# Reading the moving columns of matmuls in reverse order, with the weight tiles' places spread over 32 relations

## The chip, the cores and the metric

The kernel runs on one core of one Trainium2 chip. The metric is the device time of one execution in microseconds, as the median of several runs.

## What is computed

One decoder layer over 272 tokens (16 meta tokens and 256 of the sequence), 2048 channels wide. The part that the change touches is the feed-forward block at the end, which takes about two thirds of the time:

```python
def conv_gated_ffn(h, w_up, conv_w, conv_b, w_down):
    T = h.shape[1]
    z = h @ w_up
    zp = jnp.pad(z, ((0, 0), (CONV_WIDTH - 1, 0), (0, 0)))
    z = sum(zp[:, j:j + T] * conv_w[j] for j in range(CONV_WIDTH)) + conv_b
    a, g = jnp.split(z, 2, axis=-1)
    return (jax.nn.gelu(a) * g) @ w_down
```

`w_up` is 2048 x 11264 and `w_down` 5632 x 2048. Ahead of it stand the projections, a sparse attention, a pooling branch and an output projection, and layer norms (in `reference`: `h = layer_norm(ALPHA * h + f, ...)`).

## The kernel before

All large products run on TensorE in float32r. Each float32 operand is split into an upper part and a lower part, and a product is the sum of three matmuls: upper with upper, and each lower with the other's upper. So a block of weights of 128 x 128 costs three matmuls, and each of them loads its stationary block anew.

**Weights.** All weight tiles of 128 x 2048 come in one stream (`stream`), in the order in which they are used, each by one DMA of 1 MB into a `wraw` buffer (three of them). ScalarE writes the upper parts into a `whl` buffer (L181) and VectorE the lower parts (L182); there are three `whl` buffers of 4288 float32 places per partition. The tiles are fetched two ahead of use. Where the two parts lie in the `whl` buffer is set by a pair of places per tile (`Split`), and these set the relation of the addresses of the stationary blocks to those of the columns that stream past them. `turned` says whether the second matmul of a block takes the lower weights or the lower activations.

**Lead.** A tile that has a `lead` is stored in two pieces, the first 512 columns (four blocks) at other places than the rest, and is split by two instructions on each engine, one of 512 columns and one of 1536. A tile without one is split by two instructions of 1024 columns. Before the change every up tile has the lead `LEAD_H = (12, False)`: its first four blocks begin at place 12 in the order not turned, and its other twelve lie, counted modulo 256 bytes, 48 bytes ahead of that (place 0), in turned order.

**Up tiles.** One up tile is 128 output channels: 16 blocks, 48 matmuls, in `product` (L288 for the first of each three, L292 for the other two). The weights are stationary; the 258 columns of the normalised activations (`hp`, upper and lower parts in fixed buffers) are moving, and the result is 128 x 258 in a PSUM bank. There are 88 up tiles. The first eight work on activations before their norm (`fold`, 260 columns); the other 80 on `hp`, which makes 3840 matmuls.

**Down tiles.** In `seven` (L890 to L892) the gated activations are stationary and 512 columns of the `whl` tile are moving. Seven products of sums of blocks take the place of eight. Tiles of kind A have four products of three matmuls, tiles of kind B three; `j` counts the pairs of channel tiles that are summed in PSUM. Up and down tiles alternate from about 420 to 960 us of the span, in the order of `ffn_plan`. The scheduler of the language fixes the order of instructions on each engine when the kernel is built.

Of the kernel before, what the change touches and what calls it, by code (L numbers as in the profile page):

```python
# [23 lines left out]
NQ = T - Q0  # L24
KT = D // P
# [11 lines left out]
FOLDED = 4  # L37
# [63 lines left out]
LEAD_X, LEAD_H = (24, False), (12, False)  # L101


def lead(b):

    return LEAD_H


GATED, RIGHT, FOLD = 0, 32, 32
# [20 lines left out]
K_UP = (1, 3, 5, 7, 8, 10, 12, 15, 0, 2, 4, 6, 9, 11, 13, 14)  # L130
# [3 lines left out]
def tile_layer(ctx, tc, xt, w_first, w_proj, w_uk, w_uv, w_pool, w_o, w_up, w_down, cols, rows, rel_bias, onehot, out):  # L134
    nc = tc.nc
# [10 lines left out]
    def small():  # L146
        return pa.tile([P, 512], F32, tag="at", name="at")
# [3 lines left out]
    ps = small()  # L151
# [4 lines left out]
    stream = [w_proj[j] for j in range(8)] + [w_uk, w_uv] + [w_proj[j] for j in range(8, 24)]  # L156
    stream += [w_o[j] for j in range(KT)]
    plan = ffn_plan()
    kinds, leads, downs_at = {}, {**{i: LEAD_X for i in range(10, 18)}, **{26 + m: LEAD_H for m in (0, 1, 5)}}, {}
    for item in plan:  # L160
        if item[0] == "up":
            leads[len(stream)] = lead(2 * item[1] + item[2])
            stream.append(w_up[item[2] * FT + item[1]])
        elif item[0] == "down":
            n = PARTS[FAST]
            stream.append(w_down[sum(PARTS[:FAST]) + n // 2 + (item[2] - 1) // 2 * (n // 4) + item[3]])
        else:
            kinds[len(stream)] = item[0]
            downs_at[len(stream)] = down(item[0])
            stream.append(w_down[sum(PARTS[:item[1]]) + item[2] * (PARTS[item[1]] // 2) + item[3]])  # L170
# [3 lines left out]
    ready, raws, split, held = {}, {}, {}, []  # L174
# [103 lines left out]
        nc.scalar.activation(hi, total.to_broadcast([P, 2]), AF.Copy)  # L278
        nc.vector.tensor_tensor(lo, total.to_broadcast([P, 2]), hi.bitcast(F32), op=ALU.subtract)

    def product(ps, hl, act, lo, hi, places, ks=None, k0=0, k1=KT):

        for n in range(k0, k1):
            k = (places if ks is None else ks)[n]
            w = slice(P * places.index(k), P * places.index(k) + P)
            wh, wl = hl[:, 0, w], hl[:, 1, w]
            ah, al = act[k][:, 0, lo:hi], act[k][:, 1, lo:hi]
            nc.tensor.matmul(ps, wh, ah, start=n == 0, stop=False)  # L288
            turned = hl.early if hl.lead is not None and w.start < LEAD else hl.turned
            turn = ((wl, ah), (wh, al)) if turned else ((wh, al), (wl, ah))  # L290
            for i, (a, b) in enumerate(turn):
                nc.tensor.matmul(ps, a, b, start=False, stop=i == 1 and n == KT - 1)  # L292
# [6 lines left out]
    for k0, k1 in [(k, k + 1) for k in range(9)] + [(9, 12), (12, 15), (15, 16)]:  # L299
# [6 lines left out]
        if k0 % 6 == 0:  # L306
            hl = split_tile()
# [57 lines left out]
    ps = heads[0][0]  # L365
# [22 lines left out]
    for j in range(2):  # L388
        ps = heads[1 + j][0]
# [6 lines left out]
    ps = small()  # L396
# [482 lines left out]
    def seven(kind, part, c, j):  # L879

        hl = weights()
        n = PARTS[part] // 2
        names = (("P2", 2), ("P3", 3), ("P1", 0), ("P5", 1)) if kind == "A" else (("P7", 1), ("P6", 0), ("P4", 2))
        if j == 0:
            for name, _ in names:
                held[name] = small()
        for name, w in names:
            a, i = pairs[part][j][name]
            ps, w = held[name], slice(512 * w, 512 * w + 512)
            nc.tensor.matmul(ps, a[:, 0, i], hl[:, 0, w], start=j == 0, stop=False)  # L890
            nc.tensor.matmul(ps, a[:, 0, i], hl[:, 1, w], start=False, stop=False)  # L891
            nc.tensor.matmul(ps, a[:, 1, i], hl[:, 0, w], start=False, stop=j == n - 1)  # L892
        if j < n - 1:
            return
        c11, c12, c21, c22 = (y2[:, i, w:w + 512] for i in range(2) for w in (512 * c, 1024 + 512 * c))

        def add(to, ps):

            with tc.issue_after(split[min(state["use"] + 1, last - 1)][1]):
                nc.vector.scalar_tensor_tensor(to, to, 1.0 if part else ALPHA, ps, op0=ALU.mult, op1=ALU.add)  # L900

        if kind == "A":
            held["u"] = fp.tile([P, 512], F32, name="u", tag="u1", bufs=1, padded_shape=[P, NQ + W])
            nc.scalar.activation(held["u"], held["P1"], AF.Copy)
            held["v"] = fp.tile([P, 512], F32, name="v", tag="u2", bufs=1, padded_shape=[P, NQ + W])
            nc.scalar.activation(held["v"], held["P5"], AF.Copy)
            add(c11, held["P2"])
            add(c12, held["P3"])
            nc.gpsimd.dma_start(c11, held["u"], accum_op=ALU.add)
            nc.gpsimd.dma_start(c12, held["v"], accum_op=ALU.add)  # L910
        else:
            u, v = held["u"], held["v"]
            add(c22, v)
            nc.vector.tensor_tensor(u, u, held["P6"], op=ALU.add)  # L914
            nc.vector.tensor_tensor(v, u, held["P7"], op=ALU.add)
            add(c21, held["P4"])
            nc.gpsimd.dma_start(c12, u, accum_op=ALU.add)
            nc.gpsimd.dma_start(c21, v, accum_op=ALU.add)
            nc.gpsimd.dma_start(c22, v, accum_op=ALU.add)
# [4 lines left out]
    for item in plan:  # L924
        if item[0] in "AB":
            seven(*item)
            continue
        if item[0] == "down":
            _, part, c, g = item
            hl = weights()  # L930
            if c == 1:
                emit((last, spare)[g])
                if g == 0:
                    row_sums(last, ready[last])
            if g == 0:
                downs = [big(), big()]
            n = PARTS[part]
            for k in range(4 * g, 4 * g + 4):
                w = slice(512 * (k - 4 * g), 512 * (k - 4 * g) + 512)
                for i in range(2):  # L940
                    a, r = pairs[part][k // 2][f"a{i + 1}{k % 2 + 1}"]
                    nc.tensor.matmul(downs[i], a[:, 0, r], hl[:, 0, w], start=k == 0, stop=False)
                    nc.tensor.matmul(downs[i], a[:, 0, r], hl[:, 1, w], start=False, stop=False)
                    nc.tensor.matmul(downs[i], a[:, 1, r], hl[:, 0, w], start=False, stop=k == n - 1)
            if g == n // 4 - 1:
                for i in range(2):
                    yc = y2[:, i, 512 * c:512 * c + 512]
                    nc.vector.tensor_tensor(yc, yc, downs[i], op=ALU.add)
            continue
        _, f, half_ = item  # L950
        part = next(p for p in range(len(PARTS)) if f < sum(PARTS[:p + 1]))
        if half_ == 0:
            if f % 2 == 0:
                pair = fp.tile([P, 2, S], F32, name="za", tag="z0", bufs=3)
            both = []
        hl = weights()
        ps = big()

        b = 2 * (f - FOLDED) + half_
        upper, lower = split[state["use"] + 1]  # L960
        with tc.issue_after(lower):
            for m in turns[:(0, 5, 5, 6)[b] if 0 <= b < 4 else 0]:
                nc.vector.transpose(y[:, m, NM:], y[:, m, NM:])
                turns.remove(m)
        with tc.issue_after(upper):
            for _ in range(0 if b < 4 else 4 if b < 8 else 3):
                if moves:
                    residual(*moves.pop(0))
        if todo and f > FOLDED + half_:
            p, r = todo.pop(0)  # L970
            with behind(state["use"]):
                pairs[p].append(forms(r, len(pairs[p]), p == FAST))
        if f < FOLDED:
            k = 0
            if f + half_ == 0:
                product(ps[:, :NE], hl, folded, 0, NE, K_UP, k1=5)
                deviation()
                k = 5
            product(ps[:, :NE], hl, folded, 0, NE, K_UP, k0=k)
            with behind(state["use"]):  # L980
                while len(h_parts) < min(KT, 2 * (2 * f + half_ + 1) + 1):
                    normalise(len(h_parts))
            both.append(ps)
            if half_ == 0:
                continue
            both = [conv(i * FT + f, i, unfold(both[i]), pair[:, f % 2]) for i in range(2)]
        else:
            product(ps[:, :NQ], hl, h_parts, 0, NQ, K_UP, ks=late_last if f == FOLDED else None)
            both.append(conv(half_ * FT + f, half_, ps, pair[:, f % 2]))
            if half_ == 0:  # L990
                continue
        gate(*both)
        if part > FAST:
            a = fp.tile([P, 2, WIDE], F32R, name="gp", tag="gp", bufs=16)
            gated.append(two_parts(a[:, :, :S], both[0]))
        elif f % 2:
            todo.append((part, pair))
# [192 lines left out]
```

## Time and profile before

| | us |
|---|---|
| median of 2 runs | 1027.88 (1027.29 to 1028.48) |
| profiled execution | 1027.44 |
| its span, first to last instruction | 1025.6 |
| TensorE busy in the span | 1018.5 |
| VectorE busy | 890.5 |
| ScalarE busy | 620.1 |

The span is what the profile's rows are counted in; 1.8 us of the profiled time lie outside it. Matmuls overlap one another in the pipeline, so that the length of a single one in a row (0.28 us for 258 columns) is not what it costs. What it costs is the distance from its start to the start of the next one. In the timeline a row that ends in "x2" holds two instructions that follow one another.

### The profile page before, as it was taken

To read this page: it belongs to the slowest core of one execution; us is meant where nothing else is said; L and a number is where in the kernel's file an instruction comes from. 1 tells how busy PE (TensorE), PEld (TensorE's weight loads), DVE (VectorE), ACT (ScalarE), POOL (GpSimd) and SP (SyncE) were. 2 spreads that over 40 slices of the span, in tenths; PEclk is the share of its full clock that TensorE was granted. 3 is DMA by queue.
4 is the path that set the end of the run, shared out by engine and by line. 5 is a ranking of instruction groups with operands and counts; after the bars stand their busy time and mean duration, and the time that the engine had idled before them with its cause. 6 is when DMAs were issued, how large, how long until landed. Compare 5 with 4: busy or idle time off the path is not lost.

```text
span 1025.6 us, 19201 instructions
## 1 busy us (share of the span) xinstructions
PE 1018.5 (99%) x7644; PEld 969.4 (95%) x7644; DVE 890.5 (87%) x1401; ACT 620.1 (60%) x1000; POOL 188.4 (18%) x245
## 2 busy tenths in 40 slices
PE   9999999999999999999999999999999999999997
PEld 8999999999999999999999999999999999999986
DVE  6878668758879998999998989989899999999876
ACT  7666446645448856555666565566556656666675
POOL 1200014125430131111121111210212102120031
PEclk9999999999999999999999999999999999999998
DMA  8755643455564578979887788888888789788874
GB/s 328 257 184 206 228 154 108 138 197 168 203 205 134 189 229 249 278 283 296 281 288 259 270 275 278 277 279 298 278 272 279 292 295 289 266 290 286 290 244 138
DMA packets 59754, 250.28 MB, mean 244 GB/s; under 512 B 21734, under 2 KB 22416, under 8 KB 32656
## 3 DMA queue, kind: packets, MB, share of 16 engines
q1 hardware_dynamic: 34592, 230.42, 62.8%
q0 software_dynamic: 7888, 16.14, 8.3%
q10 hardware_dynamic: 17184, 2.49, 1.5%
q8 instruction: 60, 0.98, 0.4%
q14 instruction: 30, 0.25, 0.1%
HBM read 232.50 MB, written 2.11 MB: 229 GB/s over the span
## 4 chain that ended last, share of the span: by engine, by line
PE 71%; DVE 12%; DMA 8%; issue 4%; ACT 4%; POOL 1%; POOLq 0%; ACTq 0%; SPq 0%; DVEq 0%
PE mm L292 36%; PE mm L288 18%; DVE whl L182 6%; DMA wraw<-in_w_up 4%; DMA wraw<-in_w_down 4%; ACT whl L181 3%; PE at L891 3%; PE at L892 3%; PE at L890 3%; PE mm L363 2%; DVE y L900 1%; DVE wraw L198 1%; DVE wraw L197 1%; DVE gp L845 0%; DVE wraw L193 0%
## 5 line engine op out<-in xcount | busy, mean ns | idle before, releaser
L182 DVE TENSOR_TENSOR whl<-wraw,whl 128x1024 fp32r<-128x1024 f32 (+2 forms) x416 | 488.3, 1201 | 53.8 <-ACT whl L181 52.4
L181 ACT ACTIVATE whl<-wraw 128x1024 fp32r<-128x1024 f32 (+2 forms) x416 | 402.4, 1015 | 192.8 <-DVE wraw L198 52.1
L292 PE MATMUL mm<-hp,whl 128*128 128x258 f32 x2560 | 454.0, 280 | 0.0
L292 PEld LDWEIGHTS mm<-hp,whl 128*128 128x128 f32 x2560 | 390.9, 188 | 3.5 <-DVE whl L182 0.2
L288 PE MATMUL mm<-hp,whl 128*128 128x258 f32 x1280 | 357.6, 279 | 0.0
L288 PEld LDWEIGHTS mm<-hp,whl 128*128 128x128 f32 x1280 | 241.4, 189 | 3.1
L292 PE MATMUL mm<-xp,whl 128*128 128x256 f32 (+5 forms) x768 | 140.4, 282 | 0.0
L292 PEld LDWEIGHTS mm<-xp,whl 128*128 128x128 f32 x768 | 118.7, 189 | 0.5
L288 PE MATMUL mm<-xp,whl 128*128 128x256 f32 (+5 forms) x384 | 111.9, 292 | 0.0
L863 POOL TENSOR_TENSOR forms<-za 128x128 f32<-128x128 f32 x20 | 20.3, 1015 | 297.5 <-DVE za L839 234.5
L288 PEld LDWEIGHTS mm<-xp,whl 128*128 128x128 f32 x384 | 72.3, 188 | 1.0 <-issue 0.5
L891 PE MATMUL at<-whl,gp 128*128 128x512 f32 x180 | 70.7, 393 | 0.0
L892 PE MATMUL at<-whl,gp 128*128 128x512 f32 x180 | 70.6, 393 | 0.0
L890 PE MATMUL at<-whl,gp 128*128 128x512 f32 x180 | 68.8, 392 | 0.3 <-DVE u L914 0.3
L866 POOL TENSOR_TENSOR forms<-za 128x128 f32<-128x128 f32 x20 | 20.2, 1010 | 202.3 <-DVE za L839 190.2
L821 ACT ACTIVATE z<-mm,cv 128x256 f32<-128x256 f32 x40 | 22.3, 559 | 42.5 <-PE mm L292 42.2
L292 PE MATMUL mm<-fold,whl 128*128 128x260 f32 x256 | 45.6, 280 | 0.0
L292 PE MATMUL mm<-mixp,whl 128*128 128x258 f32 x256 | 45.5, 279 | 0.0
L292 PE MATMUL mm<-mixa,whl 128*128 128x258 f32 x256 | 45.2, 278 | 0.0
L821 ACT ACTIVATE za<-mm,cv 128x256 f32<-128x256 f32 x40 | 22.3, 558 | 35.0 <-PE mm L292 33.8
L892 PEld LDWEIGHTS at<-whl,gp 128*128 128x128 f32 x180 | 33.8, 188 | 7.4
L890 PEld LDWEIGHTS at<-whl,gp 128*128 128x128 f32 x180 | 33.5, 187 | 7.2 <-DVE u L914 1.0
(339 smaller groups left out, 1610.1 us busy)
## 6 DMA issues: line engine op xcount, KB each, us to landing
wraw<-in_w_up SPq DMA_DIRECT2D x88, 1024.0 KB, 5.2
wraw<-in_w_down SPq DMA_DIRECT2D x80, 1024.0 KB, 6.5
wraw<-in_w_proj SPq DMA_DIRECT2D x24, 1024.0 KB, 5.2
wraw<-in_w_o SPq DMA_DIRECT2D x16, 1024.0 KB, 4.9
y<-v POOLq DMA_DIRECT2D x27, 256.0 KB, 8.4
y<-u POOLq DMA_DIRECT2D x18, 256.0 KB, 5.0
wraw<-in_w_first SPq DMA_DIRECT2D x8, 304.0 KB, 5.2
x<-in_xt SPq DMA_DIRECT2D x1, 2176.0 KB, 7.8
```

Source lines behind the costliest of these rows:

```text
L181: upper = nc.scalar.activation(hl[:, 0, c], raw[:, c], AF.Copy)
L182: lower = nc.vector.tensor_tensor(hl[:, 1, c], raw[:, c], hl[:, 0, c].bitcast(F32), op=ALU.subtract)
L197: nc.vector.tensor_tensor(b12, b22, b12, op=ALU.subtract)
L288: nc.tensor.matmul(ps, wh, ah, start=n == 0, stop=False)
L292: nc.tensor.matmul(ps, a, b, start=False, stop=i == 1 and n == KT - 1)
L363: nc.tensor.matmul(ps[:m, :T], hl[:, t // 2, a0 + a:a0 + a + m], x_parts[k][:, t % 2, :], start=k == 0 and t == 0, stop=k == KT - 1 and t ...
L821: nc.scalar.activation(z, src[:, 2:NQ], AF.Identity, bias=col(C_B, j), scale=col(C_W, 3 * j + 2))
L863: nc.gpsimd.tensor_tensor(s[:, 0], a21, a22, op=ALU.add)
L866: nc.gpsimd.tensor_tensor(s[:, 3], a11, a21, op=ALU.subtract)
L890: nc.tensor.matmul(ps, a[:, 0, i], hl[:, 0, w], start=j == 0, stop=False)
L891: nc.tensor.matmul(ps, a[:, 0, i], hl[:, 1, w], start=False, stop=False)
L892: nc.tensor.matmul(ps, a[:, 1, i], hl[:, 0, w], start=False, stop=j == n - 1)
```

## The change

The change does three things, in the feed-forward block alone.

1. The 80 up tiles on `hp` read their moving columns from the last to the first, and write the columns of PSUM from the last to the first (`back=True`). The result in PSUM is the same, column by column.
2. The down tiles of odd `j` (the second and fourth pair of each four) do the same with their 512 columns: 378 matmuls.
3. Up tiles lose their lead. Tile number `b` has its upper part at place 4 x (b mod 16) and its lower part 2112 places further, in steps of 16 bytes, and 16 tiles in turned order are followed by 16 in the other. So 32 combinations come in turn; the eight tiles on `fold` get them too, and read forwards as before.

```diff
-def lead(b):
-
-    return LEAD_H
+def placed(b):
+
+    return 4 * (b % 16), 4 * (b % 16) + 2112, b // 16 % 2 == 0
...
         if item[0] == "up":
-            leads[len(stream)] = lead(2 * item[1] + item[2])
+            downs_at[len(stream)] = placed(2 * item[1] + item[2])
...
-    def product(ps, hl, act, lo, hi, places, ks=None, k0=0, k1=KT):
+    def product(ps, hl, act, lo, hi, places, ks=None, k0=0, k1=KT, back=False):
...
             ah, al = act[k][:, 0, lo:hi], act[k][:, 1, lo:hi]
+            if back:
+                ah, al = ah[:, ::-1], al[:, ::-1]
...
+        step = 1 - j % 2 * 2
         for name, w in names:
             a, i = pairs[part][j][name]
-            ps, w = held[name], slice(512 * w, 512 * w + 512)
-            nc.tensor.matmul(ps, a[:, 0, i], hl[:, 0, w], start=j == 0, stop=False)
-            nc.tensor.matmul(ps, a[:, 0, i], hl[:, 1, w], start=False, stop=False)
-            nc.tensor.matmul(ps, a[:, 1, i], hl[:, 0, w], start=False, stop=j == n - 1)
+            ps, w = held[name][:, ::step], slice(512 * w, 512 * w + 512)
+            nc.tensor.matmul(ps, a[:, 0, i], hl[:, 0, w][:, ::step], start=j == 0, stop=False)
+            nc.tensor.matmul(ps, a[:, 0, i], hl[:, 1, w][:, ::step], start=False, stop=False)
+            nc.tensor.matmul(ps, a[:, 1, i], hl[:, 0, w][:, ::step], start=False, stop=j == n - 1)
...
-            product(ps[:, :NQ], hl, h_parts, 0, NQ, K_UP, ks=late_last if f == FOLDED else None)
+            product(ps[:, NQ - 1::-1], hl, h_parts, 0, NQ, K_UP, ks=late_last if f == FOLDED else None, back=True)
```

The number of instructions stays the same on every engine, and the DMA queue's order does not change. What moves is where the split of an up tile is cut, and with it which matmul waits for the second piece. On VectorE, in the middle of the feed-forward block (near 656 us of the span), where `v<-u,at` is a sum of a down tile and `whl<-wraw,whl` the lower parts of a weight tile, the kernel before has:

```order
L915 TENSOR_TENSOR v<-u,at 128x512 [waits DMASW2_49,DMASW4_49,DMASW1_49,DVE_49]
L182 TENSOR_TENSOR whl<-wraw,whl 128x512 [waits DMAHW1_49,Activation_49]
L182 TENSOR_TENSOR whl<-wraw,whl 128x1536 [waits Activation_49]
L845 TENSOR_TENSOR gp<-za,gp 128x256 [waits Activation_49]
L845 TENSOR_TENSOR gp<-forms,gp 128x256 [waits Activation_49]
```

and the changed one, whose lines stand two or three further down:

```order
L918 TENSOR_TENSOR v<-u,at 128x512 [waits DMASW2_49,DMASW4_49,DMASW1_49,DVE_49]
L182 TENSOR_TENSOR whl<-wraw,whl 128x1024 [waits DMAHW1_49,Activation_49]
L182 TENSOR_TENSOR whl<-wraw,whl 128x1024 [waits Activation_49]
L847 TENSOR_TENSOR gp<-za,gp 128x256 [waits Activation_49]
L847 TENSOR_TENSOR gp<-forms,gp 128x256 [waits Activation_49]
```

The two pieces of the split have other sizes and stand in the same place. On TensorE, in the up tile that uses this split (the `hp` numbers are the blocks' activations), the kernel before waits for the second piece at the fifth block:

```order
L288 MATMUL mm_7917<-hp_4092,whl_7812 128x258
L292 MATMUL mm_7917<-hp_4092,whl_7812 128x258 x2
L288 MATMUL mm_7917<-hp_4098,whl_7812 128x258 [waits Activation_49]
L292 MATMUL mm_7917<-hp_4098,whl_7812 128x258 [waits DVE_49]
L292 MATMUL mm_7917<-hp_4098,whl_7812 128x258
```

and the changed one at the ninth:

```order
L290 MATMUL mm_7917<-hp_4411,whl_7812 128x258
L294 MATMUL mm_7917<-hp_4411,whl_7812 128x258 x2
L290 MATMUL mm_7917<-hp_3859,whl_7812 128x258 [waits Activation_49]
L294 MATMUL mm_7917<-hp_3859,whl_7812 128x258
L294 MATMUL mm_7917<-hp_3859,whl_7812 128x258 [waits DVE_49]
```

The wait for the second piece has moved four blocks back, and the first piece, which the tile's first matmul waits for, has grown from 512 to 1024 columns. In the changed tile the lower weights come with the third matmul of a block, which is the order that is not turned.

## Rows read from the trace of the kernel before

**Rows 1.** The page: span, busy time of the engines, TensorE's clock, up tiles' matmuls.

```profile
span 1025.6 us, 19201 instructions
PE 1018.5 (99%) x7644; PEld 969.4 (95%) x7644; DVE 890.5 (87%) x1401; ACT 620.1 (60%) x1000; POOL 188.4 (18%) x245
PEclk9999999999999999999999999999999999999998
L182 DVE TENSOR_TENSOR whl<-wraw,whl 128x1024 fp32r<-128x1024 f32 (+2 forms) x416 | 488.3, 1201 | 53.8 <-ACT whl L181 52.4
L292 PE MATMUL mm<-hp,whl 128*128 128x258 f32 x2560 | 454.0, 280 | 0.0
L288 PE MATMUL mm<-hp,whl 128*128 128x258 f32 x1280 | 357.6, 279 | 0.0
```

**Rows 2.** Stretches: length, busy us (instructions) of PE, PEld, DVE, ACT, POOL, clock, DMA.

```profile
500.00:600.00 100.00, 100.00 (x730) 94.44 (x730) 92.76 (x127) 59.45 (x83) 16.47 (x20) 1.00 0.83 276
800.00:900.00 100.00, 100.00 (x726) 94.21 (x725) 96.19 (x133) 61.06 (x88) 16.05 (x20) 1.00 0.83 284
420.00:960.00 540.00, 539.57 (x3916) 508.44 (x3916) 504.11 (x694) 325.64 (x458) 87.41 (x105) 1.00 0.85 282
```

**Rows 3.** Timeline of TensorE, one up tile: start us, length us, what.

```profile
601.07 0.28 PE L288 MATMUL mm<-hp,whl 128*128 128x258 f32 x1
...
601.42 0.28 PE L288 MATMUL mm<-hp,whl 128*128 128x258 f32 x1
...
602.50 0.28 PE L288 MATMUL mm<-hp,whl 128*128 128x258 f32 x1
...
603.57 0.28 PE L288 MATMUL mm<-hp,whl 128*128 128x258 f32 x1
...
606.34 0.28 PE L288 MATMUL mm<-hp,whl 128*128 128x258 f32 x1
...
606.69 0.39 PE L890 MATMUL at<-whl,gp 128*128 128x512 f32 x1
```

**Rows 4.** Timeline of TensorE: first matmuls of an output projection tile and its successor.

```profile
248.55 0.28 PE L288 MATMUL mm<-mixp,whl 128*128 128x258 f32 x1
...
254.09 0.28 PE L288 MATMUL mm<-mixp,whl 128*128 128x258 f32 x1
```

**Rows 5.** The same for a query tile (48 matmuls of 258 columns).

```profile
115.28 0.28 PE L288 MATMUL mm<-xp,whl 128*128 128x258 f32 x1
...
121.00 0.28 PE L288 MATMUL mm<-xp,whl 128*128 128x258 f32 x1
```

**Rows 6.** Timeline of TensorE: a down tile of kind B, nine matmuls.

```profile
769.00 0.39 PE L890 MATMUL at<-whl,right 128*128 128x512 f32 x1
769.23 0.39 PE L891 MATMUL at<-whl,right 128*128 128x512 f32 x1
769.47 0.39 PE L892 MATMUL at<-whl,right 128*128 128x512 f32 x1
769.69 0.39 PE L890 MATMUL at<-whl,right 128*128 128x512 f32 x1
...
771.07 0.28 PE L288 MATMUL mm<-hp,whl 128*128 128x258 f32 x1
```

**Rows 7.** Timeline of VectorE: both pieces of an up tile's split.

```profile
656.92 2.35 DVE L182 TENSOR_TENSOR whl<-wraw,whl 128x512 fp32r<-128x512 f32 x2
```

**Rows 8.** Timeline of TensorE: the first matmul of that tile.

```profile
658.04 0.28 PE L288 MATMUL mm<-hp,whl 128*128 128x258 f32 x1
```

**Rows 9.** Timeline of VectorE: the split's second piece alone, ahead of the tile in rows 3.

```profile
598.87 1.75 DVE L182 TENSOR_TENSOR whl<-wraw,whl 128x1536 fp32r<-128x1536 f32 x1
```

**Rows 10.** Timeline of TensorE in the attention: two matmuls in plain float32.

```profile
150.99 0.60 PE L626 MATMUL at<-pts,v 128*128 128x256 f32 x2
151.43 0.38 PE L627 MATMUL at<-pts,v 128*128 128x128 f32 x2
```

## Prediction

> **What bounds the kernel.** I read the page first. TensorE is busy in 1018.5 of the span's 1025.6 us, and its clock is granted in full, the 2.4 GHz level, in all slices but the last [rows 1]. So the time is the number of matmuls times their spacing, and a change counts only if it moves that spacing or makes TensorE wait. Then the table of stretches: between 420 and 960 us, where up and down tiles alternate, TensorE is busy for 539.57 of 540 us, but VectorE, which splits each weight tile, is busy for 504.11 of these, and for 96.19 of the 100 us from 800 on [rows 2]. There is 7% of air on VectorE and none on TensorE. Nothing else can be the bound at once.
>
> Last the timeline, for the distance from start to start. In the up tile at 601.07 us the first four blocks (12 matmuls) take 602.50 - 601.07 = 1.43 us, 0.119 us for a matmul of 258 columns. The last eight full blocks before 606.34 us (24 matmuls from 603.57 us) take 2.77 us, 0.1154 each. The whole tile, up to the down tile at 606.69, takes 5.62 us, 0.1171 each [rows 3]. At 2.4 GHz one column for each clock would be 258 / 2.4 = 0.1075 us. So there is an excess over the columns, of 8 ns at best and of 12 ns in the first four blocks. The activations are read from the same buffers in both parts, and the data type, the columns and the clock are the same. What differs is where the weights lie against the activations, and the order of the lower parts. I take this relation of addresses to be what the excess hangs on. It is a reading and not yet a proof, since the two pieces differ in order too.
>
> That step has a rule against it. The Trainium skill (SBUF — State Buffer, "Who interferes with whom") gives TensorE two independent read ports, one for the moving operand and one for loading weights, and says that "PE and ACT never wait on anyone". By that rule neither place nor direction could change anything, and the sum would be zero. The two parts of the tile in [rows 3] speak against it, 0.119 against 0.1154 us; I keep it as a rival.
>
> **The change part by part.**
>
> *Places, without a lead.* Three relations show in the trace with 258 columns. Place 0, turned, is that of an output projection tile: 254.09 - 248.55 = 5.54 us for 48 matmuls [rows 4], and twice the 2.77 us of the settled part of the up tile gives the same [rows 3]. A query tile takes 121.00 - 115.28 = 5.72 us [rows 5]. Four times the 1.43 us of the lead's blocks is 5.72 as well. The changed kernel runs through 32 relations evenly, and one of them (b = 0) is the best of the three. With no row for the others I take the mean of the three, (5.54 + 5.72 + 5.72) / 3 = 5.66 us. Against 5.62 us now that is +0.04 us for a tile, and for 88 tiles +3.5 us. The ends: all tiles at 5.54 give -0.08 x 88 = -7.0 us; all at 5.72 give +0.10 x 88 = +8.8 us. I take the mean because the 32 are a spread and not a choice.
>
> *Reversed reading.* No matmul in the trace reads or writes backwards, so there is no row for it. It does not change the number of columns. It changes which addresses of the two streams meet at which moment, as another place would. I cost the direction itself at nothing and let it sort the tiles anew among the same spacings, with the same ends. For the 378 down matmuls a row of 512 columns now takes 2.07 / 9 = 0.230 us, and the steps within the tile lie between 0.22 and 0.24 us at the row's resolution [rows 6]; at 0.01 us to either side that would be 3.8 us, but since only single steps reach these ends I take 0, with 1.5 us to either side. A price of the direction by itself is the first rival.
>
> *The cut of the split.* The first piece grows from 512 to 1024 columns; together the pieces have as many as before and as many instructions, so neither VectorE nor ScalarE has more to do. The second piece ends when it did, and is needed four blocks later, which is a gain that nothing waits for. The first piece ends later. At the tightest place that I found both pieces begin at 656.92 and end at 659.27 us [rows 7]; the piece of 1536 takes 1.75 us [rows 9], so the first ended at about 657.5, and the tile's first matmul started at 658.04 [rows 8]. A piece of 1024 takes 1.20 us on average [rows 1] and ends at 658.12, so this tile would wait 0.08 us. At the tile in [rows 3] the second piece ended at 600.62, before the tile started at 601.07, so nothing waits there. What is queued behind the waiting matmul is all of TensorE's work, so such waits add in full. At most every second tile of some 55 between 420 and 960 us can be as tight, since kinds of down tile alternate: 27 x 0.1 = 2.7 us; at least 0. I take 0.5 us, nearer to the lower end, as VectorE gains air wherever TensorE waits or slows.
>
> *DMA and the rest.* The stream's order and its bytes stay, and no queue is passed. Nothing is added.
>
> Sum: 3.5 + 0 + 0.5 = +4.0 us. The profiled execution took 1027.44 us, so 1031.4; the median of the runs is 0.4 above that execution, which gives **1032 us**. The case's own range: 1027.9 - 7.0 - 1.5 = 1019 to 1027.9 + 8.8 + 1.5 + 2.7 = 1041.
>
> **The rivals.**
>
> *Backwards is slower for every column.* Place: all 3840 + 378 reversed matmuls, in the stretch where TensorE has no air [rows 2]. They stream 3840 x 258 + 378 x 512 = 1,184,256 columns. It decides the sign from 20.6 us on (2%), which is 0.017 ns a column, or 4.5 ns for each matmul of 258: little more than what the two parts of [rows 3] differ by. As a mechanism I take that the excess over the columns, 12 ns of the tile's mean now, comes twice: 12 / 258 x 1.184 million = 55 us, 1083 us. The far end is half the rate: plain float32 matmuls, two records for 256 columns in 151.43 - 150.99 = 0.44 us, run at 0.86 ns a column [rows 10] where the up tile has 0.1171 / 258 = 0.45 ns; 0.41 x 1.184 million = 486 us, 1514 us. For it: the excess of 8 ns even at the best relation shows that the streams aren't free of a cost that grows with columns (0.230 us for 512 are 17 ns over 213 [rows 6]). Against it: the columns stay dense, each next to the last. The Trainium skill (PSUM — Partial Sum Buffer, "Specifications (TRN2)") warns that any access pattern that is not contiguous slows matmuls significantly, and puts PSUM's line at 8 bytes; no run here shows whether a descending pattern falls under that. Chance 0.15, most of it above 1048 us.
>
> *The reversal brings nearly all relations to the best.* If the streams collide less in opposite directions, every tile runs like [rows 4]: -7.0 us, and 1.5 us from the down tiles, 1019.4 us. VectorE's air of 36 us in 540 allows that. Against it: the spread was not chosen by any measurement that the rows show. Chance 0.20.
>
> *Relations don't matter, and the direction neither.* Then every tile goes on at its mean of 5.62 us, and only the cut counts: 1028.4 us. Chance 0.09, as [rows 3] speak against it.
>
> *The excess vanishes.* If all of it comes from streams that run the same way, 0.1171 falls to 0.1075 us, 36.9 us over 3840 matmuls, and 0.230 to 0.2133, 6.3 us over 378. That is 985 us on TensorE. VectorE's 504.11 us in the 540 [rows 2] would then be in the way at some tiles, so rather 990. Chance 0.05.
>
> **How the numbers follow.** The forecast has the remaining 0.51. A measurement of this kernel tells 2% from no change, which is 1007 to 1048 us. Forecast, second and third rival end inside it, with 0.80; the first ends above, except for a small part that I count with the forecast's upper end: 0.15; the fourth below: 0.05. The range takes in forecast, second and third rival. Its lower end is 1019 less what the tiles' spread leaves open, 1016; its upper end reaches past 1041 into the mild part of the first rival, 1048. Outside lie about 0.20.
>
> **What would show it.** In the profile after, the starts of up tiles should be 5.5 to 5.8 us apart without the down tile between, with a pattern that returns after 32 up tiles, and tiles with the same place but the other order should differ. Down tiles with odd j should keep 0.230 us a matmul. If the reversed tiles lie at 5.9 us or more whatever their place, the first rival is right; if they all lie at one value under 5.6, the second. If tiles of all places are equal and near 5.62, my reading of [rows 3] falls. A wait on VectorE's or ScalarE's split ahead of up tiles, over 3 us in sum, would show that I costed the cut too low. The likeliest way for me to be wrong is that a descending read has a price that no row shows.

## The result, and the profile after

| | before | changed |
|---|---|---|
| median, us | 1027.88 | 1040.51 (1039.86 to 1041.15, 2 runs) |
| ratio | | 1.0123 (95% interval 1.0079 to 1.0166) |
| span of the profiled execution, us | 1025.6 | 1038.1 |

The changed kernel is slower by 1.2%: the interval leaves out 1, and the 2% that the prediction took as the mark are not reached. The page of the changed kernel, against [rows 1]: TensorE's busy time has grown by 12.0 us with the same number of instructions, VectorE's by 0.5, and the clock is as full as before.

```profile
span 1038.1 us, 19190 instructions
PE 1030.5 (99%) x7644; PEld 981.3 (95%) x7644; DVE 891.0 (86%) x1401; ACT 621.1 (60%) x1000; POOL 186.4 (18%) x245
PEclk9999999999999999999999999999999999999999
```

In the table of stretches (length, busy us of PE, PEld, DVE, ACT, POOL with their instructions), against the third of [rows 2]:

```profile
420.00:960.00 540.00, 540.00 (x3846) 509.50 (x3845) 493.95 (x680) 319.54 (x449) 88.83 (x105) 1.00 0.83 276
```

TensorE now waits for nothing at all there, and gets through 3846 matmuls where it was 3916; VectorE has more air. So the time was lost in the spacing of matmuls and not in a wait. The timeline of TensorE in the changed kernel shows a down tile of odd `j` (12 matmuls, from 670.02 us) and an up tile (48 matmuls, from 672.83):

```profile
670.02 0.40 PE L893 MATMUL at<-whl,gp 128*128 128x512 f32 x1
...
672.83 0.28 PE L290 MATMUL mm<-hp,whl 128*128 128x258 f32 x1
...
675.71 0.28 PE L290 MATMUL mm<-hp,whl 128*128 128x258 f32 x1
...
678.59 0.40 PE L893 MATMUL at<-whl,gp 128*128 128x512 f32 x1
```

The up tile takes 5.76 us where [rows 3] had 5.62, and both of its halves take 2.88: 0.120 us a matmul from the first block to the last. The pattern of fast and slow blocks is gone. Of the 32 relations 26 give 5.75 to 5.79 us a tile. The other six lie between 5.80 and 5.87; the longest is place 4 in turned order (tiles 33 and 65), here as a second tile in the same timeline, 5.87 us:

```profile
795.55 0.28 PE L290 MATMUL mm<-hp,whl 128*128 128x258 f32 x1
...
801.42 0.40 PE L893 MATMUL at<-whl,gp 128*128 128x512 f32 x1
```

The down tile read backwards takes 2.81 / 12 = 0.234 us a matmul, against the 0.230 of [rows 6]. So the pattern that returns after 32 tiles is there, as the prediction had it (33 and 65), and the 0.230 for down tiles of odd `j` is not.

Where the 12.5 us of span went, added up over all starts in both traces: the 3840 matmuls of the 80 up tiles on `hp` took 450.7 us and take 462.3, which is +11.6; the eight tiles on `fold`, read forwards at new places, 45.7 and 46.3, +0.6; all 756 down matmuls 175.3 and 175.7, +0.4. In the last sum the reversed half is dearer by 1.2 us, and two stalls of 0.96 us together are gone that the kernel before had at down tiles (two pairs of matmuls that took 1.03 and 0.85 us in place of 0.46 each).

### The profile page after: what moved, and what is told of

Same layout as the page of the kernel before. It is cut to its first block, busy times and chain, and to the rows that moved or that the text cites. A ratio compares the mean times of both kernels' runs of the same rounds, so it can differ in the third digit from the quotient of the medians.

```text
span 1038.1 us, 19190 instructions
## 1 busy us (share of the span) xinstructions
PE 1030.5 (99%) x7644; PEld 981.3 (95%) x7644; DVE 891.0 (86%) x1401; ACT 621.1 (60%) x1000; POOL 186.4 (18%) x245
## 4 chain that ended last, share of the span: by engine, by line
PE 94%; issue 2%; DMA 1%; DVE 1%; POOL 1%; ACT 0%; SPq 0%; POOLq 0%; DVEq 0%; ACTq 0%
PE mm L294 47%; PE mm L290 24%; PE at L893 6%; PE at L895 6%; PE at L894 6%; PE mm L365 1%; DMA wraw<-in_w_down 1%; DVE whl L182 1%; DMA wraw<-in_w_first 1%; POOL gb L1012 0%; PE mm L593 0%; PE at L454 0%; PE at L628 0%; PE at L455 0%; PE at L340 0%
## 5 line engine op out<-in xcount | busy, mean ns | idle before, releaser
L294 PE MATMUL mm<-hp,whl 128*128 128x258 f32 x2560 | 465.9, 284 | 0.0
L294 PEld LDWEIGHTS mm<-hp,whl 128*128 128x128 f32 x2560 | 398.0, 190 | 3.4
L290 PE MATMUL mm<-hp,whl 128*128 128x258 f32 x1280 | 362.8, 283 | 0.0
L290 PEld LDWEIGHTS mm<-hp,whl 128*128 128x128 f32 x1280 | 242.0, 189 | 3.1
```

## The experiments

Theory, after the first reading of the result: reading backwards sets the spacing to 0.120 us, wherever the weights lie. Rival: the 32 places, or the lead that is gone, cost the time, and the direction nothing.

### places_only and reverse_only: the change in halves

Both edits are made to the changed kernel; the first block is places_only, the second reverse_only.

```diff
-            product(ps[:, NQ - 1::-1], hl, h_parts, 0, NQ, K_UP, ..., back=True)
+            product(ps[:, :NQ], hl, h_parts, 0, NQ, K_UP, ...)
...
-        step = 1 - j % 2 * 2
+        step = 1
```

> The changed kernel with all columns read forwards again: only the 32 relations of places and the missing lead are left. My theory (reading backwards sets the spacing, and the place hardly matters once it does): tiles differ by place, from 5.54 to about 5.8 us, mean about 5.65 us, total about 1030 us, clearly under the changed kernel's 1040.5. Rival (the places, not the direction, cost the 12.6 us): all 80 tiles near 5.76 us again, total about 1039 us.

```diff
-            downs_at[len(stream)] = placed(2 * item[1] + item[2])
+            leads[len(stream)] = LEAD_H
```

> The kernel before, with its places and its lead, and the reversed reading alone. My theory: the first four blocks and the other twelve, 0.119 and 0.1154 us a matmul before, both come to 0.120 us, a tile takes 5.76 us, total about 1039 us. Rival (places cost it): a tile stays at about 5.62 us, total about 1028 to 1030 us.

Measured: the places alone 1036.36 us, 1.008 of the kernel before (1.0056 to 1.0104), or +8.5 us; the direction alone 1039.73 us, 1.0111 (1.0083 to 1.0139), or +11.9 us. The two do not add up to 20.4 us: together, in the change, they cost 12.6. Read forwards, tiles differ by place. In the timeline of places_only tile 48 (place 0, not turned) takes 5.55 us and tile 58 (place 40, not turned) 5.85:

```profile
654.67 0.28 PE L290 MATMUL mm<-hp,whl 128*128 128x258 f32 x1
...
660.22 0.39 PE L893 MATMUL at<-whl,gp 128*128 128x512 f32 x1
...
736.87 0.28 PE L290 MATMUL mm<-hp,whl 128*128 128x258 f32 x1
...
742.72 0.40 PE L893 MATMUL at<-whl,gp 128*128 128x512 f32 x1
```

The mean over the 80 tiles is 5.735 us, and the middle one takes 5.755. Tile 32, whose place (0, turned) is the one that the prediction took for the best, takes 5.66:

```profile
524.30 0.28 PE L290 MATMUL mm<-hp,whl 128*128 128x258 f32 x1
...
529.96 0.40 PE L893 MATMUL at<-whl,gp 128*128 128x512 f32 x1
```

In the changed kernel, backwards, tile 58 takes 5.76 us, less than the 5.85 that it takes forwards; so do 23 of the 80 tiles:

```profile
738.47 0.28 PE L290 MATMUL mm<-hp,whl 128*128 128x258 f32 x1
...
744.23 0.40 PE L893 MATMUL at<-whl,gp 128*128 128x512 f32 x1
```

With before's places and the reversed reading alone, the timeline has both parts of the tile alike, 1.44 us for the lead's four blocks and 1.45 for the next four:

```profile
665.27 0.28 PE L290 MATMUL mm<-hp,whl 128*128 128x258 f32 x1
...
666.71 0.29 PE L290 MATMUL mm<-hp,whl 128*128 128x258 f32 x1
...
668.16 0.28 PE L290 MATMUL mm<-hp,whl 128*128 128x258 f32 x1
...
671.04 0.40 PE L893 MATMUL at<-whl,gp 128*128 128x512 f32 x1
```

So both theories have a part, and my 1030 us for the places alone was 6 us too low. Reversed reading is 0.120 us at before's places as at most others; and the rival is right that the new places, without the lead, cost time as well, when the reading is forwards. Backwards replaces the spread, 5.55 to 5.87 us, by one value in most tiles, 5.76, and that is about what the middle one of the forward tiles takes. It costs 11.9 us at before's places because those ran better than most.

### read_back and write_back: SBUF or PSUM

Both are edits of the changed kernel. In read_back only the moving operand is reversed, in write_back only PSUM; the outputs are reversed with it, so that these two serve for the time alone:

```diff
-            product(ps[:, NQ - 1::-1], hl, h_parts, 0, NQ, K_UP, ..., back=True)
+            product(ps[:, :NQ], hl, h_parts, 0, NQ, K_UP, ..., back=True)      # read_back
+            product(ps[:, NQ - 1::-1], hl, h_parts, 0, NQ, K_UP, ...)          # write_back
```

(and the same for the odd pairs of `seven`).

> The changed kernel, but PSUM is written forwards: only the moving columns are read backwards (the tokens of each product of an up tile, and the columns of down tiles of odd pairs, land in reverse order, so the output is another one). If the cost lies in the reading from SBUF: 0.120 us a matmul in all up tiles, total about 1040 us. If it lies in the descending writes to PSUM: tiles spread by place as when all is read forwards, total about 1030 us.

> The changed kernel, but the moving columns are read forwards and only PSUM is written backwards (the same reversal of tokens and columns, the output is another one). If the cost lies in the reading from SBUF: tiles spread by place between 5.54 and 5.8 us, total about 1030 us. If it lies in the descending writes to PSUM: 0.120 us a matmul in all up tiles, total about 1040 us.

Measured: 1041.7 us for the reading, 1035.5 us for the writing (one run each), which is close to the whole change (1040.5) and to places_only (1036.4). In write_back's timeline the tiles 48 and 58 take the 5.55 and 5.86 us that they take in places_only:

```profile
653.78 0.28 PE L290 MATMUL mm<-hp,whl 128*128 128x258 f32 x1
...
659.33 0.39 PE L893 MATMUL at<-whl,gp 128*128 128x512 f32 x1
...
735.98 0.28 PE L290 MATMUL mm<-hp,whl 128*128 128x258 f32 x1
...
741.84 0.40 PE L893 MATMUL at<-whl,gp 128*128 128x512 f32 x1
```

and in read_back's tile 50 takes the 5.76 us of the change:

```profile
674.18 0.28 PE L290 MATMUL mm<-hp,whl 128*128 128x258 f32 x1
...
679.94 0.40 PE L893 MATMUL at<-whl,gp 128*128 128x512 f32 x1
```

The cost of the direction lies in the reading. Descending writes to PSUM cost nothing that these runs show.

### still and narrow: is it the load of the next weights?

A matmul runs while the next stationary block is loaded, and I took the two streams to meet in SBUF. Two pairs of runs take away the other stream's walk, and then most of its length. In both pairs the forward run has before's places and lead, and the backward run those with the reversed reading (the first addition is that of the still runs, the other three lines that of the narrow ones; all four leave out most columns of the up tiles' stationary blocks, so they serve for the time alone):

```diff
             wh, wl = hl[:, 0, w], hl[:, 1, w]
+            if places is K_UP:                                                  # still
+                wh, wl = (v[:, :1].to_broadcast([P, P]) for v in (wh, wl))
...
+            few_ = 32 if 0 < n < KT - 1 and act is h_now[0] else P              # narrow
+            full, ps = (ps, ps[:few_]) if n == k0 else (full, full[:few_])
+            wh, wl = hl[:, 0, w][:, :few_], hl[:, 1, w][:, :few_]
```

> The kernel before, but each stationary block of an up tile is one column read 128 times (the products of the up tiles are other ones): the load of the next block no longer walks through the buffer. If the excess over 0.1075 us comes from that walk meeting the moving stream: the two parts of the tile, 0.119 and 0.1154 us, come to one value. If the relation of places works in another way: they stay apart. To be compared with still_back.

> The same with the reversed reading (before's places and lead, one column read 128 times as stationary block). If reading backwards costs because of the meeting of two walks (my theory): the spacing is that of still_fwd, within 1 ns. Rival, a descending read costs 4 to 5 ns for 258 columns by itself: 0.120 us or more, 4 ns above still_fwd.

> The kernel before, but in blocks 2 to 15 of the up tiles on hp the stationary block has 32 columns in place of 128 (the other 96 output channels get only the first and the last block), so the load beside each matmul is a quarter as long. If the excess over 0.1075 us comes from the load: it falls to a quarter or so, 0.110 us a matmul, and the places cease to matter. If it belongs to the moving read alone: 0.115 to 0.120 us as before. To be compared with narrow_back.

> The same with the reversed reading (before's places and lead). If the flat 0.120 us of the reversed reading comes from the load of the stationary block beside it: 0.110 to 0.113 us, within 1 ns or so of narrow_fwd. If a descending read has a price by itself, which still_back now speaks for: 0.120 us, 4 ns or more above narrow_fwd.

Measured, one run each: 1027.4 and 1038.0 us with still weights, 1026.8 and 1039.2 us with narrow ones. In still_back's timeline a tile takes 2.89 and 2.88 us for its halves, 0.120 a matmul; the same tile in still_fwd takes 669.74 - 664.14 = 5.60 us, 0.1167, and its two parts have come together: the lead's four blocks take 665.54 - 664.14 = 1.40 us, the other twelve 4.20, both 0.1167 a matmul.

```profile
671.45 0.28 PE L292 MATMUL mm<-hp,whl 128*128 128x258 f32 x1
...
674.34 0.28 PE L292 MATMUL mm<-hp,whl 128*128 128x258 f32 x1
...
677.22 0.39 PE L895 MATMUL at<-whl,gp 128*128 128x512 f32 x1
```

```profile
664.14 0.28 PE L290 MATMUL mm<-hp,whl 128*128 128x258 f32 x1
...
665.54 0.28 PE L290 MATMUL mm<-hp,whl 128*128 128x258 f32 x1
...
669.74 0.40 PE L892 MATMUL at<-whl,gp 128*128 128x512 f32 x1
```

The loads of narrow_fwd are really shorter, as its groups of instructions show (the second number after the bar is the mean length in ns): 108 ns for 32 columns, 188 for 128, which is more than the quarter that I had expected.

```profile
L296 PEld LDWEIGHTS mm<-hp,whl 128*32 128x32 f32 x2240 | 241.7, 108 | 20.2
L296 PEld LDWEIGHTS mm<-hp,whl 128*128 128x128 f32 x320 | 49.5, 188 | 3.2
```

But blocks 9 to 15 of its tile, 21 matmuls, take 671.19 - 668.76 = 2.43 us, 0.1157 each, as in [rows 3], and the same blocks of narrow_back 677.51 - 674.99 = 2.52, 0.120 each:

```profile
668.76 0.28 PE L292 MATMUL mm<-hp,whl 128*32 128x258 f32 x1
...
671.19 0.28 PE L292 MATMUL mm<-hp,whl 128*128 128x258 f32 x1
```

```profile
674.99 0.28 PE L294 MATMUL mm<-hp,whl 128*32 128x258 f32 x1
...
677.51 0.29 PE L294 MATMUL mm<-hp,whl 128*128 128x258 f32 x1
```

For the reversed reading my explanation falls in both forms: its 0.120 us stay when the load does not walk, and when it is a quarter as wide. For the forward reading a part of it may stand. By the sign that I had set, the two parts of the tile come to one value when the load stands still, which speaks for the walk of the load as what set them apart. But the tile as a whole keeps its excess over 0.1075 us, 5.60 us in place of 5.62, and 32 columns of walk are enough to keep the parts apart (narrow_fwd: 0.119 and 0.1157 us). All but a little of the excess, and all of the 0.120 us, stay without the load's length or walk.

### pairs_back: columns or the walk

Against reverse_only, two columns are kept together; PSUM is written in the same order (that line is left out here):

```diff
-                ah, al = ah[:, ::-1], al[:, ::-1]
+                ah, al = (v.rearrange("p (a b) -> p a b", b=2)[:, ::-1] for v in (ah, al))
```

> Reversed reading with before's places and lead, but the 258 columns of up tiles are walked as 129 pairs: the pairs descend, the two columns of a pair ascend (PSUM is written in the same order, the result is the reference's). Down tiles of odd pairs go column by column as in the change. If the price lies in the descending order of the walk: 0.120 us flat again, total about 1039 us. If it lies in the step of minus one from column to column: the spacing differs from 0.120, towards 0.1155, or, if short runs have a price of their own, far above.

Measured: 1039.66 us, and 5.77 us for a tile (664.03 to 669.80 in its timeline), as reverse_only. A step of minus one from column to column is not what costs, nor does a pattern of runs of two cost anything more. What the two have in common is that the walk as a whole goes down. No run reads upwards in another order than column after column, so whether any order but the plain one takes 0.120 us stays open.

```profile
664.03 0.28 PE L290 MATMUL mm<-hp,whl 128*128 128x258 f32 x1
...
669.80 0.40 PE L893 MATMUL at<-whl,gp 128*128 128x512 f32 x1
```

### no_lead, best_place and short_lead: forwards, in search of 0.1156 us throughout

places_only seemed to name good places, and the settled part of [rows 3] another one. Three kernels read forwards give every up tile one of them: no_lead takes before's lead away, best_place is places_only with `placed` returning `0, 2112, False`, and short_lead halves the lead (no_lead and short_lead are edits of the kernel before):

```diff
-            leads[len(stream)] = lead(2 * item[1] + item[2])
+            pass                                                                # no_lead
...
-LEAD = 512
+LEAD = 256                                                                      # short_lead
```

> The kernel before, read forwards, without the lead: all 16 blocks of an up tile at place 0 and 2048, turned, as in an output projection tile. If place alone sets the spacing: 0.1156 us in all blocks, 5.55 us a tile in place of 5.62, total 1021 to 1023 us. If the first blocks then wait for the longer first piece of the split: waits ahead of up tiles, total 1025 us or above.

> All up tiles at the best of the 32 relations that places_only showed (place 0 and 2112, not turned, 0.1157 us a matmul), read forwards, without a lead. If what a tile costs is a property of its relation and not of the tiles around it: 5.55 us a tile, total 1021 to 1023 us. If a tile's spacing hung on its neighbours' places: it moves away from 0.1157, total 1026 us or above.

> The kernel before, read forwards, with a lead of 256 columns (two blocks) in place of 512. no_lead ran at 0.122 us on the same places as before's last twelve blocks at 0.1156, so the lead's blocks seem to decide into which of two patterns the rest falls. If two blocks at the other place are enough for that: blocks 3 to 16 settle at 0.1156, 5.57 to 5.60 us a tile, total 1023 to 1026 us. If not: 0.122 us and 5.83 us a tile, total about 1041 us.

Measured: 1040.69 us (1.0124, 1.0089 to 1.0158), 1042.35 us (1.014, 1.0108 to 1.0172) and 1031.83 us (1.0045, 1.0029 to 1.0062). All three are slower than before, the first two about as slow as the change. In no_lead it is no wait: its TensorE is busy for 540.00 of the 540 us from 420 to 960, and the first up tile on `hp` is the only one with waits, 1.1 us. It is the spacing. In no_lead's timeline blocks 9 to 15, 21 matmuls at the places (modulo 256 bytes) and in the order in which before had 0.1154 us, take 671.26 - 668.69 = 2.57 us, 0.122 each:

```profile
668.69 0.29 PE L288 MATMUL mm<-hp,whl 128*128 128x258 f32 x1
...
671.26 0.29 PE L288 MATMUL mm<-hp,whl 128*128 128x258 f32 x1
```

The addresses of no_lead and before agree only modulo 256 bytes, but best_place shows the switch at one place within one run: tile 12, among up tiles only, takes 5.55 us, and tile 49, after a down tile, 5.85. Tiles 9 to 16 all take 5.55 to 5.56 us, and they go through all three `whl` buffers, so it isn't a buffer either. Nor is it the down tile as such: tile 22, at 440.74 us, follows one as well and takes 5.54, and in no_lead it is the tiles among up tiles only that take 5.87.

```profile
369.28 0.28 PE L290 MATMUL mm<-hp,whl 128*128 128x258 f32 x1
...
374.83 0.28 PE L290 MATMUL mm<-hp,whl 128*128 128x258 f32 x1
...
440.74 0.28 PE L290 MATMUL mm<-hp,whl 128*128 128x258 f32 x1
...
446.28 0.39 PE L893 MATMUL at<-whl,right 128*128 128x512 f32 x1
...
662.79 0.28 PE L290 MATMUL mm<-hp,whl 128*128 128x258 f32 x1
...
668.64 0.39 PE L893 MATMUL at<-whl,gp 128*128 128x512 f32 x1
```

There are values between the two as well: three of no_lead's tiles between 410 and 441 us take 0.118 us a matmul.

In short_lead tile 48 settles (5.60 us). The tile from 710.16 us does not: its eighth matmul waits 0.55 us for VectorE's second piece (the bracket in the row says so), and behind the wait blocks 9 to 15 take 716.43 - 713.87 = 2.56 us, 0.122 each:

```profile
652.15 0.28 PE L288 MATMUL mm<-hp,whl 128*128 128x258 f32 x1
...
657.75 0.39 PE L890 MATMUL at<-whl,gp 128*128 128x512 f32 x1
...
711.70 0.51 PE L292 MATMUL mm<-hp,whl 128*128 128x258 f32 x2 [0.55 <-DVE whl L182]
...
713.87 0.29 PE L288 MATMUL mm<-hp,whl 128*128 128x258 f32 x1
...
716.43 0.29 PE L288 MATMUL mm<-hp,whl 128*128 128x258 f32 x1
```

short_lead has such single waits in six up tiles, the longest about 0.7 us, and all six run at 0.122 us behind the wait. Of the other 59 tiles from 452 us on, 58 settle at 5.59 to 5.60 us (tile 51, with one late matmul of 0.02 us, takes 5.86). The kernel before does the same once, with its lead of four blocks: in the tile from 640.93 us the fifth block takes 642.99 - 642.37 = 0.62 us in place of 0.35, and blocks 9 to 15 take 646.63 - 644.07 = 2.56 us, 0.122 each.

```profile
642.37 0.28 PE L288 MATMUL mm<-hp,whl 128*128 128x258 f32 x1
...
642.99 0.28 PE L288 MATMUL mm<-hp,whl 128*128 128x258 f32 x1
...
644.07 0.29 PE L288 MATMUL mm<-hp,whl 128*128 128x258 f32 x1
...
646.63 0.29 PE L288 MATMUL mm<-hp,whl 128*128 128x258 f32 x1
```

So the blocks at the start of a tile bring the rest into the faster pattern, and a wait behind them throws it into the slower one; no run adds a wait to test this, it is read from these seven tiles. Four blocks do it in every tile of before from 447 us on that has no wait; two do it in nearly all from 452 us on, but not in the nine tiles among up tiles only (from 347.68 us, 5.82 to 5.83 us each). A wait can also end the slower pattern: in best_place the first tile on `hp` runs at 0.122 us up to its waits, and the tile after it settles at 0.1156. No version that beats the kernel before came out of this.

## Why the prediction was right or wrong

**The bound** was right: TensorE's spacing was the whole of it, and neither VectorE nor a DMA had a part.

**The sign, the size and the range.** The sign was right. +12.6 us was measured where +4.0 was forecast, in the range (1016 to 1048) and at the upper end of the case's own, 1041. The sum had two terms that were both too small. That 1040.5 still lies under 1041 is luck: the up tiles cost 12.2 us in the span (11.6 and 0.6), where the case's upper end had 8.8; it also had 2.7 us of waits, and these did not come.

**Places without a lead**, forecast +3.5 us. Alone they cost 8.5 (places_only). The step that mis-sized it is the mean of three rows, 5.66 us a tile: it weighed the best spacing with a third, and over the 32 relations it is about a tenth; the mean is 5.735, and more than half of the 80 tiles lie above the upper end, 5.72, that I had taken for all. Place 0, turned, which was to be the best, took 5.66 us there and not 5.54.

**Reversed reading**, forecast 0. This is the step that failed in kind: "I cost the direction itself at nothing and let it sort the tiles anew among the same spacings". It does not sort, it levels: 0.120 us in most relations, with the lead or without. Alone it costs 11.9 us. The first rival came nearest, with a direction that counts whatever the place, but it was not a surcharge either: it doubled the excess, where the excess became 12.5 ns throughout against 8 to 12, and at 23 of 80 tiles backwards is the faster way. Its 12 ns were also misread: they are those of the first four blocks, and the tile's mean is 0.1171 - 0.1075 = 9.6 ns, which by its own mechanism gives 44 us and not 55. Its rule of thumb (all tiles at 5.9 us or more) would have called it absent. The second rival, all tiles at the best, went the wrong way, and with it the fourth, an excess that vanishes; the third, in which neither place nor direction counts, falls with the 8.5 and the 11.9 us.

**How the two combine** was not asked in the prediction. A term for places and one for direction were added as if independent. They are not: once the read descends, the place matters little (5.76 us in 26 of 32 relations), so the cost is near the larger one, not the sum.

**The lead.** I read the two spacings in [rows 3] as two relations of addresses. no_lead shows 0.122 us at the relation of the faster one, and best_place both at one relation, so the relation alone does not set the spacing; what ran before, and a wait in the tile, decide between settled patterns. The caution in the prediction ("the two pieces differ in order too") named a difference, but not this one.

**The cut of the split**, forecast +0.5 us of waits. None appeared between 420 and 960 us: TensorE fills 540.00 of 540 us. As it slowed by 2%, VectorE had more air, which the prediction had as the reason for the low end.

**Ports and PSUM.** The Trainium skill (SBUF — State Buffer, "Who interferes with whom") has TensorE's two read ports independent, and narrow_fwd and narrow_back agree with that: a load of 108 in place of 188 ns changes neither 0.1157 nor 0.120. still_fwd fits it less well: a load that stands still brings the tile's parts from 0.119 and 0.1154 us to 0.1167 both. That "PE and ACT never wait on anyone" does not explain why one and the same place runs at 0.1156 or 0.122 us; here the measurement decides. The rule of the Trainium skill (PSUM — Partial Sum Buffer, "Specifications (TRN2)"), that a pattern that is not contiguous slows matmuls, does not reach a dense descending one: write_back costs nothing against places_only.

**What stays open.** Why a descending read takes 0.120 us, and what the two forward patterns are in hardware, no run here shows. That what happened before sets them, and not the place alone, is shown; that the moving read settles into a rhythm with something else is only a picture of it.

## What to carry to other kernels

Read the moving operand of float32r matmuls upwards where the kernel has reached a good spacing: downwards took 0.120 us for 258 columns at most places, against 0.1156 at best and 0.122 at worst upwards, while writing PSUM downwards cost nothing. A single wait in the middle of a tile can cost more than itself, since the rest of the seven tiles that had one ran at 0.122 us. A spacing that is read off one tile is not a property of its addresses; put the candidate into all tiles and measure that, since a scan that changes the place from tile to tile showed 5.55 us for a place that gave 5.85 us when all tiles had it. Two changes that act on the same spacing are not to be added.

## What was unexpected of the hardware

Matmuls of one shape at the same addresses and the full clock run in stable patterns of different spacing, 0.1156 us and 0.122 us from start to start above all. A few blocks at another place ahead of them can bring the faster one, and a wait in the tile was followed by the slower one to its end, in all seven such tiles of short_lead and before behind 447 us. The 0.120 us of a descending read do not depend on the width of the stationary block (32 or 128 columns), on whether its columns are all one address, or on pairs of columns being kept upright, and hold in 26 of 32 relations of places; for 512 columns it is 0.234 against 0.230 us.
